# Gating branch of a two-layer RWKV-7 / gMLP step interleaved with the first pair's front, and triangles inverted by blocks of 16 with quadrant matmuls

## The chip, the core and the metric

The kernel runs on one core of one Trainium2 chip. The metric is the time of one execution on the device, in microseconds, as the median of several runs; three runs of the kernel before took 3381.95, 3382.55 and 3396.24 us.

## What is computed

Two layers over 640 tokens (128 of a context, 512 of a latent grid), D_MODEL = 1024, 16 heads of 64. What matters of the reference, per layer (`z = h @ w_in` after a modulated RMSNorm):

```python
def _rwkv_step(S, inp):
    r, w, k, v, neg_kk, b = inp
    sa = jnp.einsum('dbhij,dbhj->dbhi', S, neg_kk)
    S = S * w[..., None, :] + sa[..., :, None] * b[..., None, :] + v[..., :, None] * k[..., None, :]
    return S, jnp.einsum('dbhij,dbhj->dbhi', S, r)
...
    wd = jnp.tanh(wd.reshape(B, T, N_DIR, W_LORA).astype(f32))
    w_logit = p['w0'][l][:, None, None, :] + jnp.einsum('btdr,drc->dbtc', wd, p['w_up'][l])
    decay = jnp.exp(-DECAY_SCALE * jax.nn.sigmoid(w_logit))
...
def chunk_mlp_branch(zu, zv, p, l):
    B, T, _ = zu.shape
    u = jax.nn.gelu(zu)
    v = jax.nn.gelu(zv).astype(jnp.float32)
    mu = jnp.mean(v, axis=-1, keepdims=True)
    var = jnp.mean(jnp.square(v - mu), axis=-1, keepdims=True)
    v = (v - mu) * lax.rsqrt(var + EPS) * p['ln_v_g'][l]
    vc = v.reshape(B, T // CHUNK, CHUNK, H_B, HEAD_B)
    s = jnp.einsum('hpq,bnqhc->bnphc', p['w_s'][l], vc) + jnp.transpose(p['b_s'][l])[:, :, None]
    y = u * s.reshape(B, T, D_B).astype(u.dtype)
    return y @ p['w_branch_b'][l]
...
    mixed = (jax.nn.sigmoid(z_ga) * y_a + jax.nn.sigmoid(z_gb) * y_b) @ p['w_out'][l]
    x = x + g1 * mixed
    h2 = rmsnorm(x, p['norm2_g'][l]) * (1 + sc2) + sh2
    x = x + g2 * (jnp.square(jax.nn.relu(h2 @ p['w1'][l])) @ p['w2'][l])
```

The scan runs forward and backward. The kernel does it by chunks of L = 64 tokens, 10 chunks for each of two directions, for 8 pairs of heads.

## The kernel before

All activations lie as 8 tiles of 128 channels by 640 tokens. A float32 product is done as three passes over operands split in a high and a low part: `load_w` (L97) brings 256 KB of weights through SyncE's queue, ScalarE writes the high part (`hi`, L101), VectorE or GpSimdE the rest (`lo`, L103), and `dense` (L116) runs two `load_w` and 2 x 24 = 48 matmuls of 320 columns (L111, tile `dps`). Such a set of 48 is called a dense block here.

A layer goes through these stages in the program:

- `p1` (L393 to L519): the low-rank inputs (`lah`, `lal`), the gate's v (L491, four quarters of 120 matmuls of 256 columns, evicted with Gelu, tiles `v0` to `v4`), eight dense blocks for u (L504, evicted with Gelu to `uts`), 40 low-rank units in between (`lora_units`, L449: six matmuls, two ScalarE evictions of 320 columns at L468 or L470, one store to `ld`), the normalisation of v, and eight spatial products (`spatial`, L438: five matmuls with `wst`, then VectorE, result to `bd`). In layer 0 it also reduces 32 columns of the modulation (`mod_col`, L162), two reductions of 1024 elements each on VectorE (L168), which the loads of 512 KB feed.
- the front of pair 0, alone: `krv(0, 0, 1, 2)`, `run(0, ...)`, two `gate` blocks.
- the loop over the pairs: `back(i)` (ten recurrence steps, the tiles `pu`), and in between the steps pieces of `front(i + 1)`, dense blocks for k, r, v of the pairs to come (`krv`) and dense blocks of the output gates (`gate`). `SP` (L35) says how many pieces go where: `n` per step, `gn` gate blocks per pair. `mark`, `adv` and `high_priority` give the pieces of a front a higher priority; from that and the program's order the framework orders each engine's queue. Every engine then runs its queue in order.
- `branch_b` (the gate's product with `w_branch_b`), then output projections and the feed-forward part.

`front(i)` (L581) makes, per direction, the decay sums (`cum`, `E`), the operands `LA`, `BK`, then g = BK^T LA per chunk and head (L644, tile `g`), whose masked parts go to `GR`, `LA`, `D` and `TT`. The lower triangles of the 64x64 blocks are inverted: the two 32x32 diagonal blocks of all 20 chunks and both heads at once on VectorE, by substitution over s = 1 to 30 (L673 to L678, tiles `D`, `X`: one multiply and one add each of (31 - s) x s elements), then transposed (`XT`, `XN`, L692 and L694), copied to `TT` (L698), and merged with the off-diagonal block by 2 x 40 small matmuls (tiles `pw`, L705 and L715). `lnexp` (L551) issues Ln and Exp under one table set that is loaded ahead (`pre`).

```python
for s in range(1, 31):
    n = 31 - s
    t3 = tm[:, 0:n * s].rearrange("p (a b) -> p a b", b=s)
    nc.vector.tensor_tensor(t3, AA[:, s + 1:32, s:s + 1].to_broadcast([128, n, s]),
                            X[:, s:s + 1, 0:s].to_broadcast([128, n, s]), ALU.mult)
    nc.vector.tensor_tensor(X[:, s + 1:32, 0:s], X[:, s + 1:32, 0:s], t3, ALU.add)
```

## Time and profile before

| | us |
|---|---|
| median of three runs | 3382.55 |
| the profiled execution | 3388.05 |
| its span, first to last instruction | 3386.3 |
| TensorE busy (matmuls) | 3159.4 |
| VectorE busy | 2145.6 |
| ScalarE busy | 1511.6 |
| GpSimdE busy | 612.4 |
| mean granted TensorE clock, of full | 0.942 |

The profile's page names engines PE (matmuls), PEld (weight loads), DVE (VectorE), ACT (ScalarE), POOL (GpSimdE), SP (SyncE, whose queue issues the loads and stores). L111 is line 111 of the kernel before. The times of matmuls are modelled: they overlap, so a busy share near one is not the engine at its peak; how long a run of matmuls takes is read from the start of the first to the start of what follows. PEclk is the mean granted clock of a stretch; its two levels are 1.2 and 2.4 GHz. The stages of the text are windows in microseconds from the span's start: layer 0's opening 74.6 to 247.4, pair 0's front to 368.0, the loop to its last recurrence matmul at 1074.2; layer 1's 1754.1, 1914.6, 2036.0 and 2743.7.

### The profile page before, as it was taken

The page shows a single profiled execution, that of the slowest core. Times are in us where ns is not written, and L with a number is a line of the kernel's source. Part 1 is how long each engine was busy: PE and PEld are TensorE (multiplying, and loading weights), DVE is VectorE, ACT ScalarE, POOL GpSimd, SP SyncE. Part 2 cuts the span into 40 slices and gives each one's busy share as a digit, 9 for nine tenths or more (in the row PEclk, how much of TensorE's full clock was granted, in tenths as well). Part 3 has the DMA queues.
Part 4 walks back from the last instruction along what each step waited for, and adds up shares of the span by engine and source line. Part 5 has one row for each costly group of instructions (what it writes and reads, how often), then busy time and mean ns, then how long its engine had stood idle before and what let it go on. Part 6 is the DMA issues. An engine that isn't in the chain of part 4 may idle for free.

```text
span 3386.3 us, 66312 instructions
## 1 busy us (share of the span) xinstructions
PE 3159.4 (93%) x26160; PEld 2862.3 (85%) x26160; DVE 2145.6 (63%) x4147; ACT 1511.6 (45%) x3268; POOL 612.4 (18%) x616
## 2 busy tenths in 40 slices
PE   7998899999999999999989979999999999999998
PEld 7897677777778989999989967777777789899998
DVE  7777778887785469933353487788787735532234
ACT  5444445554445354224254434445544543541432
POOL 3004333333231000000000133333323210000000
PEclk8998889998899999999999989899889999999999
DMA  6683112221224536622344522122222245222223
GB/s 210 220 291 102 56 61 72 77 74 61 66 77 138 199 104 205 216 83 75 99 135 139 188 75 66 56 73 77 68 68 72 86 137 184 84 76 75 75 75 106
DMA packets 215671, 372.73 MB, mean 110 GB/s; under 512 B 63680, under 2 KB 72000, under 8 KB 215360
## 3 DMA queue, kind: packets, MB, share of 16 engines
q1 hardware_dynamic: 215360, 368.49, 33.8%
q8 instruction: 206, 3.38, 0.4%
q14 instruction: 105, 0.86, 0.1%
HBM read 288.41 MB, written 63.31 MB: 104 GB/s over the span
## 4 chain that ended last, share of the span: by engine, by line
PE 65%; DVE 18%; DMA 5%; issue 5%; ACT 4%; POOL 3%; SPq 1%; DVEq 0%; ACTq 0%; POOLq 0%
PE dps L111 40%; PE g L644 4%; DMA wada<-in_wada 3%; PE dps L256 3%; PE dps L491 2%; DVE X L678 2%; DVE D L676 2%; PE pu L776 2%; DVE wjunk L168 2%; PE pu L757 2%; PE pu L789 1%; PE pu L795 1%; PE pu L751 1%; DVE lo L103 1%; POOL BK L625 1%
## 5 line engine op out<-in xcount | busy, mean ns | idle before, releaser
L101 ACT ACTIVATE hi<-raw 128x512 fp32r<-128x512 f32 x630 | 397.2, 632 | 1025.6 <-PE dps L111 864.0
L103 DVE TENSOR_TENSOR lo<-raw,hi 128x512 fp32r<-128x512 f32 x550 | 392.1, 714 | 545.9 <-ACT hi L101 526.7
L111 PE MATMUL dps<-ah,hi 128*128 128x320 f32 x2768 | 686.9, 324 | 8.4 <-ACT up L468 5.4
L111 PE MATMUL dps<-ah,lo 128*128 128x320 f32 x2768 | 674.3, 321 | 14.5 <-DVE lo L103 14.5
L111 PE MATMUL dps<-al,hi 128*128 128x320 f32 x2768 | 674.9, 321 | 0.0
L111 PEld LDWEIGHTS dps<-ah,lo 128*128 128x128 f32 x2768 | 474.4, 193 | 29.5 <-DVE lo L103 16.5
L111 PEld LDWEIGHTS dps<-ah,hi 128*128 128x128 f32 x2768 | 474.2, 192 | 28.2 <-ACT up L468 6.0
L111 PEld LDWEIGHTS dps<-al,hi 128*128 128x128 f32 x2768 | 473.9, 192 | 12.7 <-issue 0.8
L168 DVE CUSTOM_DVE_ANT_0 wjunk<-wada,sc 128x1024 f32<-128x1024 f32 x176 | 220.9, 1255 | 33.2 <-DMA wada<-in_wada 30.9
L785 POOL TENSOR_TENSOR sw<-SV,wc 64x128 f32<-64x128 f32 x288 | 150.7, 523 | 439.0 <-DVE SV L803 422.5
L644 PE MATMUL g<-LA,BK 64*128 64x128 f32 x1280 | 193.6, 332 | 32.9 <-DVE LA L656 15.9
L103 POOL TENSOR_TENSOR lo<-raw,hi 128x512 fp32r<-128x512 f32 x80 | 123.2, 1540 | 543.6 <-ACT hi L101 491.8
L644 PEld LDWEIGHTS g<-LA,BK 64*128 64x128 f32 x1280 | 162.0, 226 | 64.6 <-issue 22.2
L111 PE MATMUL dps<-fh,lo 128*128 128x320 f32 x896 | 205.5, 311 | 6.2 <-DVE lo L103 6.0
L111 PE MATMUL dps<-fh,hi 128*128 128x320 f32 x896 | 204.7, 310 | 0.0
L111 PE MATMUL dps<-fl,hi 128*128 128x320 f32 x896 | 204.5, 309 | 0.0
L676 DVE TENSOR_TENSOR D<-AA,X 128x30 f32<-128x30 f32 (+14 forms) x480 | 178.1, 371 | 21.6 <-POOL X L671 11.7
L678 DVE TENSOR_TENSOR X<-X,D 128x30 f32<-128x30 f32 (+14 forms) x480 | 179.9, 375 | 11.3
L249 POOL TENSOR_TENSOR al<-nt,ah 128x320 fp32r<-128x320 f32 x24 | 25.2, 1053 | 728.1 <-ACT ah L248 727.0
L111 PEld LDWEIGHTS dps<-fh,lo 128*128 128x128 f32 x896 | 150.0, 188 | 7.9 <-DVE lo L103 7.8
L625 POOL TENSOR_TENSOR BK<-ta,cum 64x640 f32<-64x640 f32 x64 | 125.8, 1966 | 141.4 <-DVE ta L616 116.3
L111 PEld LDWEIGHTS dps<-fh,hi 128*128 128x128 f32 x896 | 150.3, 188 | 0.0
(293 smaller groups left out, 5798.1 us busy)
## 6 DMA issues: line engine op xcount, KB each, us to landing
raw<-in_w SPq DMA_DIRECT2D x280, 256.0 KB, 2.6
raw<-in_win SPq DMA_DIRECT2D x234, 256.0 KB, 2.7
wada<-in_wada SPq DMA_DIRECT2D x88, 512.0 KB, 4.1
ld<-up SPq DMA_DIRECT2D x80, 320.0 KB, 3.6
th<-ld SPq DMA_DIRECT2D x32, 320.0 KB, 2.9
ta<-ld SPq DMA_DIRECT2D x32, 320.0 KB, 3.0
gd<-spill SPq DMA_DIRECT2D x32, 320.0 KB, 2.3
raw<-in_wo SPq DMA_DIRECT2D x40, 256.0 KB, 2.6
```

Source lines behind the costliest of these rows:

```text
L101: nc.scalar.activation(hi, raw, AF.Copy)
L103: (eng or nc.vector).tensor_tensor(lo, raw, hi.bitcast(F32), ALU.subtract)
L111: nc.tensor.matmul(ps[:, n, 0:HT], w[:, k * 128:(k + 1) * 128], xk[:, n * HT:(n + 1) * HT], start=(first and k == 0 and j == 0), stop=(las ...
L168: nc.vector.tensor_tensor_reduce(junk, wt, sc_cur[0][:, v, :], 1.0, 0.0, ALU.mult, ALU.add, mods[l][:, j, v:v + 1])
L256: nc.tensor.matmul(ps[:, n, 0:HT], w[:, k * 128:(k + 1) * 128], x[:, 4 * kb + k, hs(n)], start=(kb == 0 and k == 0 and j == 0), stop=(kb = ...
L491: nc.tensor.matmul(o, x[:, k, tk * 128:(tk + 1) * 128], w[:, kk * 256:(kk + 1) * 256], start=(k == 0 and j == 0 and tk % 2 == 0), stop=(k ...
L625: nc.gpsimd.tensor_tensor(b[s, c, 1 - h, :], rt[s], e[s], ALU.mult)
L644: nc.tensor.matmul(gs[h][:, c - c0, :], b[s, c, :, :].rearrange("p x t -> p (x t)"), la[s, c, h:h + 2, :].rearrange("p x t -> p (x t)"), s ...
L676: nc.vector.tensor_tensor(t3, AA[:, s + 1:32, s:s + 1].to_broadcast([128, n, s]), X[:, s:s + 1, 0:s].to_broadcast([128, n, s]), ALU.mult)
L678: nc.vector.tensor_tensor(X[:, s + 1:32, 0:s], X[:, s + 1:32, 0:s], t3, ALU.add)
L757: nc.tensor.matmul(pu[s, d, 3, :], SV[:, us[d], h, :], GR[d][:, cs[d], h, :], start=False, stop=True, skip_group_check=True)
L785: nc.gpsimd.tensor_tensor(sw[s], SV[s, both, h, :], wcu[s, both].unsqueeze(2).to_broadcast([64, 2, L]), ALU.mult)
```

## The change

- **The opening.** `p1` moves behind the definitions of front and back. It now computes the low-rank inputs, then k, r, v of pair 0 (`krv(0, 0, 1, 2)`), 20 low-rank units in one piece, the first five pieces of pair 0's front, then the four quarters of v with five low-rank units and three pieces of the front after each; then the normalisation, k and r of pair 1, and the spatial products with two pieces of the front ahead of each. The weights and biases of a spatial product come one head at a time, through one buffer each (`wst`, `bsb`), instead of all heads at once.
- **The eight u blocks** become fillers: they stand first in the list that `gate` takes from, are spilled to `zud` without Gelu, and `gn` now places 24 of them in the loop instead of 16 in front and loop. The Gelu of u, its product with the spatial result and the split for `branch_b` (`branch_b_prep`) stand in the steps of the last pair.
- **Layer 0's late modulation** is done in the loop by halves of 512 elements, one half column a step (`mod_halves`, `mod_some(1)`), 64 loads of 256 KB through one buffer (`wah`).
- **The inversion.** VectorE's substitution runs over the 16x16 diagonal blocks only, s = 1 to 14, two blocks in one instruction of 2 x (15 - s) x s elements. The off-diagonal 16x16 block of each 32x32 block comes from 80 matmuls of 16 columns (`pwa`), a masked add into `wq`, 80 matmuls (`pwt`) and 40 matmuls (`pwn`) of 32 columns, each on one of the four 32x32 quadrants; then the old merge to 64.
- Some tiles of the odd pairs move to a pool that opens after the opening (`rwb`), and the scratch memory for dynamic DMA gets smaller, to make room.

```diff
-SP = {'n': (3, 2, 1, 2, 2, 1, 0, 0, 3, 1), ... 'gn': (2, 2, 2, 1, 2, 2, 2, 1)}
+SP = {'n': (3, 2, 1, 2, 2, 1, 1, 1, 1, 1), ... 'gn': (2, 3, 3, 3, 3, 3, 3, 2)}
...
+        idq = G([128, 32], "idq")
+        for q in range(4):
+            nc.vector.tensor_copy(idq[32 * q:32 * q + 32, :], ident[32 * q:32 * q + 32, 32 * q:32 * q + 32])
+        low16 = G([128, 1], "low16")
+        nc.vector.tensor_reduce(low16, idq[:, 16:32], mybir.AxisListType.X, ALU.add)
...
+                    wq = rw.tile([128, 20, 32], F32, tag="wq", name="wq")
+                    nc.gpsimd.tensor_copy(wq[:, :, 16:32], idq[:, 16:32].unsqueeze(1).to_broadcast([128, 20, 16]))
...
-                        for s in range(1, 31):
...
+                        for s in range(1, 15):
+                            n = 15 - s
+                            t4 = tm[:, 0:2 * n * s].rearrange("p (a t s) -> p a t s", a=2, s=s)
+                            nc.vector.tensor_tensor(t4, xb[:, :, s + 1:16, s:s + 1].to_broadcast([128, 2, n, s]),
+                                                    xb[:, :, s:s + 1, 0:s].to_broadcast([128, 2, n, s]), ALU.mult)
+                            nc.vector.tensor_tensor(xb[:, :, s + 1:16, 0:s], xb[:, :, s + 1:16, 0:s], t4, ALU.add)
...
+                        quads = [slice(32 * q, 32 * q + 32) for q in range(4)]
+                        pw = psr.tile([128, 20, 16], F32, tag="g", name="pwa")
+                        for u in range(20):
+                            for s in quads:
+                                nc.tensor.matmul(pw[s, u, :], D[s, u, :], XN[s, u, 0:16], start=True, stop=True)
+                        nc.vector.scalar_tensor_tensor(wq[:, :, 0:16], pw, low16, idq[:, 0:16].unsqueeze(1).to_broadcast([128, 20, 16]), ALU.mult, ALU.add)
+                        yield "W"
+                        for x in range(2):
+                            us = slice(10 * x, 10 * x + 10)
+                            pt = psr.tile([128, 10, 32], F32, tag="g", name="pwt")
+                            pn = psr.tile([128, 10, 32], F32, tag="g", name="pwn")
+                            for u in range(10 * x, 10 * x + 10):
+                                for s in quads:
+                                    nc.tensor.matmul(pt[s, u - 10 * x, :], wq[s, u, :], XT[s, u, :], start=True, stop=True)
+                            for u in range(10 * x, 10 * x + 10):
+                                for s in quads[0::2]:
+                                    nc.tensor.matmul(pn[s, u - 10 * x, :], XT[s, u, :], wq[s, u, :], start=True, stop=True)
+                            for s in quads[0::2]:
+                                nc.scalar.activation(XN[s, us, :], pn[s], AF.Copy)
+                            for q, s in enumerate(quads):
+                                o = 32 * (q % 2)
+                                nc.scalar.activation(TT[s, us, o:o + 32], pt[s], AF.Copy)
+                        yield "V"
...
+                    fillers = [(27 + m, zud[m]) for m in range(8)] + [(43 + 8 * x + m, gd[x, m]) for x in range(2) for m in range(8)]
...
+                        krv(0, 0, 1, 2)
...
+                        def spatial(h):
+                            ws = p1.tile([128, 128], F32, tag="wst", name="wst")
+                            nc.sync.dma_start(ws, I["wsT"][l, :, h])
+                            bs = p1.tile([128, 128], F32, tag="bsb", name="bsb")
+                            nc.sync.dma_start(bs, I["bs"][l:l + 1, h].to_broadcast([128, 128]))
...
+                        lora(20)
+                        run(0, 5)
+                        for q in range(4):
...
+                            lora(5)
+                            run(0, 3)
...
+                        krv(1, 0, 1)
+                        for h in range(NK):
+                            run(0, 2)
+                            spatial(h)
+                        run(0)
...
+                            nc.scalar.activation(u, u, AF.Gelu_apprx_tanh)
+                            nc.vector.tensor_tensor(t, t, u, ALU.mult)
                             split(bh[m], bl[m], t)
...
+                                for j in range(32):
+                                    wt = rwb.tile([128, 512], F32, tag="wah", name="wah")
+                                    nc.sync.dma_start(wt, I["wada"][0, 16 + j, :, w])
...
+                                mod_some(1)
+                                if i == NPAIR - 1:
+                                    if step == 0:
+                                        branch_b_tiles()
+                                    if step < NK:
+                                        branch_b_prep(step)
```

How the queues read at three places. First TensorE in layer 0, where pair 0's first g matmuls stand (tile `g`; line numbers are those of each kernel). Before:

```order
L111 MATMUL dps<-ah,hi 128x320 x2
L111 MATMUL dps<-al,hi 128x320 x2
L644 MATMUL g<-LA_2793,BK_2794 128x128 x8
L111 MATMUL dps<-ah,lo 128x320 x2
L111 MATMUL dps<-ah,hi 128x320 x2
```

And now:

```order
L862 MATMUL dps<-hi,al 128x256
L862 MATMUL dps<-hi,ah 128x256
L526 MATMUL g<-LA_1157,BK_1158 128x128 x8
L862 MATMUL dps<-hi,ah 128x256
L862 MATMUL dps<-lo,ah 128x256
```

The g matmuls of pair 0 stood among gate blocks (320 columns), after the whole opening; now they stand among the matmuls of the gate's v (256 columns, now L862), inside it.

Second SyncE's queue in layer 0, at the spatial products (`wst` weights, `bsb` biases, `bd<-st` the store of a result). Before, where both were loaded, once:

```order
L303 DMA zs_589<-zraw 32x448
L304 DMA zs_589<-zraw 32x448
L426 DMA bsb<-in_bs 128x1024
L428 DMA wst<-in_wsT 128x1024
L99 DMA raw<-in_win 128x512
```

And now:

```order
L811 DMA bsb<-in_bs 128x128
L809 DMA wst<-in_wsT 128x128
L820 DMA bd<-st 128x640
L811 DMA bsb<-in_bs 128x128
L809 DMA wst<-in_wsT 128x128
L820 DMA bd<-st 128x640
L811 DMA bsb<-in_bs 128x128
L104 DMA raw<-in_win 128x512
```

One load of each for all heads became a load of each per head, between the stores of the heads before. On TensorE the spatial products of six heads stand there one behind the other, with no dense matmul between.

Third ScalarE in the loop, at the normalisation of a pair's result (`YD<-pg` is Ln, `YD<-YD` is Exp). Before:

```order
L718 ACTIVATE TT_3559<-pw_4506 32x10x32 x2
L553 ACTIVATE YD<-pg,c_gn 128x320 x2
L733 ACTIVATE SV<-trv 64x3x64
L553 ACTIVATE YD<-YD 128x640
L735 ACTIVATE SV<-trv 64x4x64
```

And now:

```order
L106 ACTIVATE hi<-raw 128x512
L435 ACT_TABLE_LOAD
L435 ACTIVATE YD<-pg,c_gn 128x320 x2
L435 ACT_TABLE_LOAD
L435 ACTIVATE YD<-YD 128x640
L106 ACTIVATE hi<-raw 128x512
```

Ln and Exp followed each other under one table set; now each has a table load ahead of it, here and at the normalisation of kk in every front. The whole queue holds 29 table loads before and 91 now.

## Rows read from the trace of the kernel before

**Rows 1.** Busy time of each engine by stage, with counts, clock, DMA share, GB/s.

```profile
74.60:247.40 172.80, 162.22 (x1185) 155.72 (x1186) 131.22 (x218) 83.91 (x169) 1.36 (x1) 0.98 0.77 257
247.40:368.00 120.60, 92.67 (x706) 86.12 (x704) 98.00 (x159) 49.40 (x103) 47.40 (x39) 0.85 0.30 94
368.00:1074.20 706.20, 660.51 (x6815) 538.16 (x6817) 538.68 (x1185) 350.34 (x931) 229.25 (x242) 0.92 0.24 76
...
1754.10:1914.60 160.50, 159.46 (x1185) 155.09 (x1186) 51.86 (x83) 77.07 (x157) 1.29 (x1) 0.98 0.47 161
1914.60:2036.00 121.40, 92.68 (x706) 86.00 (x704) 98.03 (x159) 49.38 (x103) 47.85 (x39) 0.84 0.29 93
2036.00:2743.70 707.70, 661.40 (x6815) 538.78 (x6817) 540.12 (x1185) 350.48 (x931) 226.69 (x242) 0.92 0.24 75
```

**Rows 2.** Waits of TensorE, pair 0's front of layer 1: total us, times, longest.

```profile
PE pw L705 <- DVE XN L694: 16.5, 1, 16.5
```

**Rows 3.** Waits of TensorE, loop of layer 1.

```profile
PE pw L705 <- DVE XN L694: 11.1, 7, 3.4
```

**Rows 4.** The page's costliest groups: the substitution; busy us, mean ns, idle before.

```profile
L676 DVE TENSOR_TENSOR D<-AA,X 128x30 f32<-128x30 f32 (+14 forms) x480 | 178.1, 371 | 21.6 <-POOL X L671 11.7
L678 DVE TENSOR_TENSOR X<-X,D 128x30 f32<-128x30 f32 (+14 forms) x480 | 179.9, 375 | 11.3
```

**Rows 5.** The chain that ended last, whole span: start us, us, engine, tile, line.

```profile
363.08 2.37 PE pw L705 x80
...
1772.78 14.58 PE dps L491 x120
...
1889.05 7.04 PE dps L111 x48
```

**Rows 6.** The same chain, 1875 to 1912 us (opening of layer 1).

```profile
1896.09 0.89 PE dps L463 x6
...
1899.61 1.11 PE dps L443 x10
```

**Rows 7.** The same chain, 2300 to 2400 us (loop of layer 1).

```profile
2306.69 0.55 PE pg L578 x2
...
2345.53 1.79 PE g L644 x15
...
2356.32 0.38 PE pu L757 x8
...
2394.24 1.45 PE pw L705 x80
```

**Rows 8.** TensorE in order of time, 2313 to 2326 us: start, us, instruction.

```profile
2315.75 1.04 PE L730 MATMUL trv<-ident,vp 128*128 128x128 f32 x8
```

**Rows 9.** TensorE in order of time, 2368 to 2382 us.

```profile
2373.82 0.41 PE L111 MATMUL dps<-al,hi 128*128 128x320 f32 x1
2374.16 0.45 PE L789 MATMUL pu<-psb,TT 64*64 64x64 f32 x8
```

**Rows 10.** Costliest groups of ScalarE, whole span: the low-rank evictions.

```profile
L468 ACT ACTIVATE up<-hps,dpar 128x320 f32<-128x320 f32 x64 | 30.7, 543 | 0.2
```

**Rows 11.** DMA issues, whole span: count, KB each, median us to landing.

```profile
SV<-in_st SPq DMA_DIRECT2D x64, 16.0 KB, 2.1
...
wst<-in_wsT SPq DMA_DIRECT2D x2, 512.0 KB, 4.7
```

**Rows 12.** VectorE's substitution by shape, loop of layer 1.

```profile
L678 DVE TENSOR_TENSOR X<-X,D 128x108 f32<-128x108 f32 x14 | 4.1, 293 | 0.4
...
L676 DVE TENSOR_TENSOR D<-AA,X 128x30 f32<-128x30 f32 x14 | 2.9, 205 | 4.9 <-POOL X L671 4.7
```

**Rows 13.** ScalarE in order of time, 1078.5 to 1085 us.

```profile
1080.24 1.28 ACT L553 ACT_TABLE_LOAD   x1
1081.54 0.95 ACT L553 ACTIVATE YD<-pg,c_gn 128x320 f32<-128x320 f32 x2
```

**Rows 14.** The page's costliest groups: the reductions of the modulation.

```profile
L168 DVE CUSTOM_DVE_ANT_0 wjunk<-wada,sc 128x1024 f32<-128x1024 f32 x176 | 220.9, 1255 | 33.2 <-DMA wada<-in_wada 30.9
```

More of the change, by code (lines that the diff above doesn't have):

```diff
@@ L699, in front @@
-                        yield "mrg"
+                        nc.vector.transpose(XN.rearrange("p u j -> p j u"), xa.rearrange("p t j -> p j t"))
+                        nc.scalar.activation(vp[1][:, 64:64 + T], v[:, ::-1], AF.Copy)
+                        bon = kd[0]
+                        nc.vector.tensor_tensor(bon, kd[0], kd[1], ALU.add)
+                        nc.vector.scalar_tensor_tensor(bon, bon, P[:, RKC + i:RKC + i + 1], r, ALU.mult, ALU.mult)
+                        ps = dense_ps()
@@ new lines, in front @@
+                        f32mm(ps, ones_b, bon)
+                        nc.vector.tensor_tensor(pv(bon), ps[:, :, 0:HT], pv(v), ALU.mult)
+                        nc.sync.dma_start(bvd[i], bon)
+                        yield "bon"
+                        quads = [slice(32 * q, 32 * q + 32) for q in range(4)]
[3 more added lines that the diff above has]
+                                nc.tensor.matmul(pw[s, u, :], D[s, u, :], XN[s, u, 0:16], start=True, stop=True)
@@ L714, in front @@
                                     s = slice(64 * h + 32, 64 * h + 64)
-                                    nc.tensor.matmul(pw[x][64 * h:64 * h + 32, u - 10 * x, :], wsb[s, u * 32:(u + 1) * 32], XT[s, u, :], start=True, stop=True)
+                                    nc.tensor.matmul(pw[x][64 * h:64 * h + 32, u - 10 * x, :], wsb[s, u * 32:(u + 1) * 32], TT[s, u, 32:64], start=True, stop=True)
                             for h in range(2):
@@ L843, in drain @@
                             pass
-                    gates = [(x, m) for x in range(2) for m in range(8)]
+                    fillers = [(27 + m, zud[m]) for m in range(8)] + [(43 + 8 * x + m, gd[x, m]) for x in range(2) for m in range(8)]
                     gi = 0
@@ L854, in gate @@
                         nonlocal gi
-                        for _ in range(min(n, len(gates) - gi)):
+                        for _ in range(min(n, len(fillers) - gi)):
                             mark("gate")
-                            gate_block(*gates[gi])
+                            spill_block(*fillers[gi])
                             gi += 1
```

380 lines of the change are left out of this document (182 added, 198 removed).

## The prediction, made blind

> **What bounds the kernel now.** I first cut the span into stages by when each stage's own matmuls run, and asked for the busy time of every engine in each [rows 1]. A layer has an opening (gating and low-rank work), a front of pair 0 that nothing accompanies, a loop over the pairs up to the last recurrence matmul, and a rest that the change hardly touches. The reader is to see three regimes. In the opening of layer 1 TensorE is busy 159.46 of 160.50 us at a clock of 0.98. In pair 0's front it is busy 92.68 of 121.40 at 0.84. In the loop it is busy 661.40 of 707.70 at 0.92, while VectorE has 540.12. So the loop looks TensorE-bound, but a busy matmul there is not one at its peak.
>
> The waits say who holds TensorE. In the front one wait of 16.5 us stands out: the merge waits for the transposes behind the 30-step substitution on VectorE [rows 2]. In the loop the same wait comes 7 times but costs 11.1 us in all [rows 3], of the 46 us that TensorE idles. The substitution is 480 multiplies and 480 adds, 178.1 + 179.9 us over 16 pairs, 22.4 us a pair [rows 4].
>
> Then unit prices, at the upper of the two clock levels. A dense block is 48 matmuls in 7.04 us, 0.147 each, and a quarter of the gate's v 14.58 [rows 5]; a low-rank unit 0.89, a spatial product 1.11 [rows 6]. In the loop a recurrence group of 8 takes 0.38, 15 g matmuls 1.79, two ones_b products 0.55, 80 merge matmuls 1.45 [rows 7]; 8 transposes 1.04 [rows 8]. One dense matmul between two recurrence groups takes 0.34 from its start to the next start [rows 9], so an insertion costs some 0.19 beyond the matmul, about 0.1 of it already inside the 0.38.
>
> With the counts of the program's order, the loop of a layer (first trv to last pu) needs: 1603 dense x 0.147 = 235; 392 recurrence groups x 0.38 = 149; 560 g instructions x 0.119 = 67; 316 transposes x 0.13 = 41; 108 ones_b instructions x 0.275 = 30; 14 merges x 1.45 = 20; some 300 insertions x 0.1 = 30. That is **572 us, against 706.20 and 707.70 measured: 134 us of slack**. It holds the 46 us of idle time, the lower clock, and gaps too short to be listed.
>
> **Part by part, per layer.**
> *Opening and pair 0's front.* Now 172.80 + 120.60 = 293.4 us in layer 0 and 160.50 + 121.40 = 281.9 in layer 1. The eight u blocks and two gate blocks leave (10 x 7.04 = 70 us of TensorE). What stays, run as one stretch: five k, r, v blocks 35; 40 low-rank units 36; the gate's v 58; 8 spatial products 9; pair 0's g 10, transposes 3, ones_b products 2, merges 3, new quadrant matmuls 4 (below); 90 shape changes 9. Sum 169. To it I add stalls. (a) The first 20 low-rank units now stand in one piece: ScalarE needs two evictions of 0.543 each [rows 10], 1.09 a unit against TensorE's 0.89, and has weight splits and pair 0's exponentials in the same queue: 12 us. (b) The spatial weights come through one buffer, so every product waits for a load issued after the product before it. The nearest rows are loads of 16 KB, 2.1 us, and the old one of 512 KB, 4.7 [rows 11]; 64 KB is nearer the first, so I take 2.4 with the issue, and six of eight products stand without dense work between: 14 us (bounds 12 and 28). (c) Of the front's other idle time, 28.7 - 16.5 = 12 us [rows 1, 2], half: 6. Together **201 us**, a gain of 92 and 81. The 16.5 us wait goes because the low-rank and v matmuls lie over the front; if that cover fell short, the shorter substitution still takes some 15 off it.
>
> *The inversion.* VectorE loses 22.4 us a pair and gains 28 instructions of 28 to 112 elements at 0.205 (128x30) to 0.293 (128x108) [rows 12], 7.3 us, and one masked add, 0.4: 14.7 us less a pair. In the loop this lies beside TensorE, and I count only what follows from it (the slack). TensorE gains 80 matmuls of 16 columns and 120 of 32, two instructions each: 400. The merge has two row groups at work and takes 1.45 us for 80 instructions [rows 7], 18 ns each; 320 of the new ones have four quadrants, so I take half, 9 ns: 2.9 + 1.4 = **4.3 us a pair**. Bounds: 3, and at the lower clock 2.37 us for 80 [rows 5], 11.9.
>
> The merge's rows show two row groups sharing one PSUM bank without taking turns. The Trainium skill (TensorEngine Tiling (Array Packing), Gotcha 1: PSUM Pressure) says that different row tiles cannot access the same PSUM bank simultaneously, and here all four write one bank. By it the new matmuls would take turns, and the sum would be that of the fourth rival; the merge's rate speaks against it.
>
> *The loop.* It takes on 454 more dense matmuls (by the order, 2057 against 1603), 67 us, and 7 x 4.3 = 30 of quadrants; shape changes stay. TensorE's own need goes from 572 to **669**. The slack I take at 70 instead of 134: VectorE, busy 538.68 of 706.20, loses some 85, so masks and weight splits come sooner, and nearly every pair has 288 dense matmuls to lay over waits instead of 182 to 240. In the opening of layer 1, where dense work is plentiful, 1 us is idle [rows 1]; the bounds are 15 and 134. Loop: 739, **33 us more** than now.
>
> *ScalarE.* The order holds 91 table loads instead of 29: Ln and Exp, which shared one set, now load one each, four loads a pair. A load takes 1.28 us, and the next instruction starts 0.02 after it [rows 13]: 5.1 us a pair in a loop where ScalarE is busy 350 of 706. I cost it at nothing beyond the slack, because dense matmuls stand behind nearly every recurrence step; uncovered, it is the third rival. The Trainium skill (ScalarE: Activation LUTs, What ACT_TABLE_LOAD costs) puts a drain of about 1.38 us on top of each load, by which the third rival would end at 3476, slower; the trace has no room for such a drain.
>
> *Rest.* 74 dense matmuls pass from before to after the last recurrence: 11 us. Layer 0's late modulation moves into the loop, 64 halves with two reductions of half of 1.255 [rows 14], 80 us of VectorE that lay under the opening's matmuls and takes back most of what the substitution freed there: 8 us (0 to 25; its loads, through one buffer, stand in SP's queue ahead of weight loads, which is in the 25).
>
> **Sum.** Layer 0: -92 + 33 + 11 + 8 = -40. Layer 1: -81 + 33 + 11 = -37. The profiled execution took 3388.05 us, 5.5 above the median of 3382.55; less 77 it is 3311, and the median **3306 us**. With the slack between 45 and 100 and the opening 10 either way, the forecast's own range is 3236 to 3386.
>
> **The rivals.**
> 1. *The loop swallows the moved blocks.* If VectorE is what keeps TensorE waiting there, the slack falls to about 20: 2 x 50 less, **3206 us**. For it: VectorE's 76% in the loop. Against: short waits on recurrence and evictions stay. Chance 0.20.
> 2. *The loop's slack stays.* It is TensorE's in-order queue waiting for the recurrence and for g's evictions, which a dense block placed elsewhere in the order does not cover; then everything moved in is paid in full: 2 x 64 more, **3434 us**, slower. It decides from a slack of 108 a layer. For it: only 11 of the 46 us belong to the substitution [rows 3]. Chance 0.10.
> 3. *Table loads on the chain.* All 64 in the pairs delay the recurrence or its normalisation: 64 x 1.28 = 82 us more, **3388 us**, no change. Against: ScalarE is half idle. Chance 0.10.
> 4. *The quadrants take turns.* Two row groups together reach 18 ns, so one at a time takes 36: 400 x 36 ns = 14.5 us a pair instead of 4.3, on the bound engine, 163 more: **3469 us**. Chance 0.04.
>
> **How the numbers follow.** The forecast has the remaining 0.56. A measurement of this kernel tells about 0.5%, 17 us, from no change: 3366 and 3400 are the borders. Faster: nine tenths of 0.56, the first rival and a little of the third, 0.72. Same: the rest of the forecast and most of the third, 0.14. Slower: the second and the fourth, 0.14. The range 3215 to 3395 leaves out the two slow rivals and a third of the first, 0.2.
>
> **What would show it.** Opening and front together near 201 us, with gaps of 2 to 3 us ahead of the spatial products; no long wait ahead of the quadrant matmuls, and 80 of them in well under 1.45 us; 28 substitution instructions of 0.2 to 0.3; a loop of 730 to 750 us with a granted clock above 0.92. A loop over 780, or quadrant bursts of 3 us, would make the prediction wrong on one side, a loop of 700 on the other.

## The result, and the profile after

The changed kernel takes 3837.76 us (median of four runs, 3830.84 to 3881.17) where the kernel before takes 3382.25: a ratio of 1.136, 95% interval 1.127 to 1.145. It is 455 us slower; the forecast was 77 us faster, and the range ended at 3395. The profiled execution took 3881.17 us, the longest of the four, so its trace is 493 us longer than the one of before: 471 in the stages below, 22 in the rest.

The page of the changed kernel: span; busy time, share and instructions of TensorE and VectorE; the granted clock in 40 slices.

```profile
span 3879.5 us, 79239 instructions
PE 3537.9 (91%) x32560; PEld 3162.2 (82%) x32560; DVE 1986.0 (51%) x3773; ACT 1635.2 (42%) x3476; POOL 609.7 (16%) x650
PEclk8787868787777999999997878788889889999999
```

VectorE has lost work, as the change meant it to (1986 us busy against 2145.6). TensorE's clock is low in both openings and loops (the first 13 slices, and slices 22 to 34). The stages, cut as in [rows 1], but with opening and front as one window, since the change interleaves them:

```profile
74.60:355.90 281.30, 230.16 (x1761) 201.24 (x1761) 98.41 (x162) 118.26 (x250) 29.91 (x30) 0.76 0.32 108
355.90:1337.00 981.10, 892.75 (x10069) 741.59 (x10069) 592.66 (x1268) 422.32 (x1050) 251.17 (x266) 0.79 0.26 83
2025.00:2302.50 277.50, 224.40 (x1761) 195.90 (x1760) 99.00 (x162) 115.50 (x242) 30.31 (x24) 0.78 0.33 110
2302.50:3222.70 920.20, 837.28 (x10069) 700.16 (x10070) 498.04 (x1000) 419.63 (x1046) 234.82 (x265) 0.86 0.22 69
```

From such a row three parts can be worked out: idle time (length less PE busy), what the low clock cost (length x (1 - PEclk), since the lower level is half speed), and the rest, TensorE's work at full clock. The page gives the clock to two places, so the last two are good to some 5 us in a loop.

| stage | | length | idle | clock | rest |
|---|---|---|---|---|---|
| opening and front, layer 0 | before | 293.4 | 38.5 | 21.5 | 233 |
| | after | 281.3 | 51.1 | 67.5 | 163 |
| opening and front, layer 1 | before | 281.9 | 29.8 | 22.6 | 230 |
| | after | 277.5 | 53.1 | 61.1 | 163 |
| loop, layer 0 | before | 706.2 | 45.7 | 56.5 | 604 |
| | after | 981.1 | 88.4 | 206.0 | 687 |
| loop, layer 1 | before | 707.7 | 46.3 | 56.6 | 605 |
| | after | 920.2 | 82.9 | 128.8 | 709 |

The rest moved as forecast: 66 to 71 us left each opening, 83 to 104 came into each loop. What was not forecast is the idle time and, more than that, the clock: 0.79 and 0.86 in the loops where the prediction wanted above 0.92. The loop's slack did not fall from 134 to 70 us a layer; idle time and clock alone went from 103 to 212 in layer 1 and to 294 in layer 0.

Where the clock is low, one pattern stands out. TensorE in order of time, changed kernel, layer 1's opening (start, us, instruction, count):

```profile
2221.39 0.31 PE L592 MATMUL pwt<-XT,wq 32*32 32x32 f32 x2
2221.63 0.64 PE L116 MATMUL dps<-al,hi 128*128 128x320 f32 x1
2222.20 0.31 PE L592 MATMUL pwt<-XT,wq 32*32 32x32 f32 x2
2222.44 0.64 PE L116 MATMUL dps<-al,hi 128*128 128x320 f32 x1
```

and three windows there: the low-rank units in one piece, pair 0's quadrants and merge, the spatial products.

```profile
2056.20:2076.70 20.50, 13.95 (x60) 12.55 (x60) 5.25 (x6) 11.30 (x24) 0.88 (x1) 0.50 0.77 267
...
2208.30:2247.40 39.10, 37.65 (x506) 25.79 (x508) 4.95 (x7) 12.02 (x23) 1.69 (x2) 0.52 0.14 44
2255.60:2295.30 39.70, 21.23 (x101) 18.90 (x100) 9.88 (x16) 8.51 (x11) 1.52 (x2) 0.61 0.28 86
```

One dense matmul and two quadrant instructions take 0.81 us from one start to the next; in a block a dense matmul takes 0.147 at the upper clock [rows 5] and 0.27 at the lower (2683.99 to 2686.65 us of this trace). One pair's quadrants and the first third of its merge, priced at 4.3 and 1 us, take 39 here together with some 50 dense matmuls, at a clock of 0.52 and with TensorE "busy" nearly throughout.

### The profile page after: what moved, and what is told of

Same layout as the page of the kernel before. It is cut to its first block, busy times and chain, and to the rows that moved or that the text cites. A ratio compares the mean times of both kernels' runs of the same rounds, so it can differ in the third digit from the quotient of the medians.

```text
span 3879.5 us, 79239 instructions
## 1 busy us (share of the span) xinstructions
PE 3537.9 (91%) x32560; PEld 3162.2 (82%) x32560; DVE 1986.0 (51%) x3773; ACT 1635.2 (42%) x3476; POOL 609.7 (16%) x650
## 5 line engine op out<-in xcount | busy, mean ns | idle before, releaser
L116 PE MATMUL dps<-ah,lo 128*128 128x320 f32 x2768 | 717.7, 337 | 61.2 <-DVE lo L108 59.6
L116 PE MATMUL dps<-ah,hi 128*128 128x320 f32 x2768 | 727.7, 340 | 4.7 <-ACT hi L106 1.8
L116 PE MATMUL dps<-al,hi 128*128 128x320 f32 x2768 | 726.2, 339 | 0.0
L116 PEld LDWEIGHTS dps<-ah,lo 128*128 128x128 f32 x2768 | 501.8, 203 | 81.5 <-DVE lo L108 63.6
L116 PEld LDWEIGHTS dps<-ah,hi 128*128 128x128 f32 x2768 | 501.1, 203 | 27.5 <-ACT hi L106 3.3
L116 PEld LDWEIGHTS dps<-al,hi 128*128 128x128 f32 x2768 | 500.9, 202 | 20.9 <-issue 2.9
L694 DVE COPY SV<-pu 64x128 f32<-64x128 f32 x160 | 46.8, 294 | 249.7 <-ACT SV L693 223.8
L116 PEld LDWEIGHTS dps<-fl,hi 128*128 128x128 f32 x896 | 150.3, 188 | 0.0
L173 DVE CUSTOM_DVE_ANT_0 wjunk<-wada,sc 128x1024 f32<-128x1024 f32 x112 | 142.7, 1274 | 14.2 <-DMA wada<-in_wada 13.0
L706 DVE TENSOR_TENSOR SV<-pu,sw 64x128 f32<-64x128 f32 x256 | 73.6, 288 | 136.3 <-PE pu L698 130.3
```

What stands on the lines that cost most here:

```text
L116: nc.tensor.matmul(ps[:, n, 0:HT], w[:, k * 128:(k + 1) * 128], xk[:, n * HT:(n + 1) * HT], start=(first and k == 0 and j == 0), stop=(las ...
L173: nc.vector.tensor_tensor_reduce(junk, wt, sc_cur[0][:, v, :], 1.0, 0.0, ALU.mult, ALU.add, mods[l][:, j, v:v + 1])
L694: nc.vector.tensor_copy(SV[64:128, both, 1, :], pu[64:128, :, 1, :])
L706: nc.vector.tensor_tensor(dst, pu[s, :, 2, :], sw[s], ALU.add)
```

## The experiments

"Half-clock time" in the expectations is the time at the lower of the clock's two levels, twice the clock column above. "Pieces" are stretches of merge and quadrant matmuls in TensorE's program order with no other matmul between. All ratios are to the kernel before, run on the same chip.

| run | median us | ratio, 95% interval | pieces |
|---|---|---|---|
| before | 3382 to 3389 | 1 | 32 |
| the change | 3837.76 | 1.136 (1.127 to 1.145) | 276 |
| change, old inversion | 3575.73 | 1.056 (1.054 to 1.059) | 32 |
| before, quadrants | 3851.00 | 1.138 (1.134 to 1.141) | 596 |
| before, quadrants in fixed bursts | 3699.02 | 1.093 (1.090 to 1.095) | 112 |
| before, quadrants in priority bursts | 3512.05 | 1.038 (1.034 to 1.041) | 80 |
| change, priority bursts | 3745.36 | 1.108 (1.104 to 1.112) | 81 |
| change, short substitution only | 3643.61 | 1.077 (1.074 to 1.081) | 220 |
| before, short substitution only | 3494.51 | 1.032 (1.030 to 1.034) | 248 |
| the same, merge in bursts | 3374.94 | 0.995 (0.992 to 0.997) | 32 |
| before, merge in bursts | 3368.49 | 0.994 (0.992 to 0.996) | 30 |

### Is it the inversion or the schedule?

The changed kernel with the 30-step substitution back (the lines of the kernel before, same pieces of a front, no quadrants):

```diff
-                        for s in range(1, 15):
...
+                        for s in range(1, 31):
...
-                        pw = psr.tile([128, 20, 16], F32, tag="g", name="pwa")
...
```

> The changed kernel with the old inversion: VectorE's 30-step substitution and no quadrant matmuls; the schedule, the pieces of a front and everything else stay as in the change. Theory A (the quadrant matmuls and the merge are a stretch of small matmuls in which the granted clock falls to its lower level, about 25 to 35 us in each pair of the changed kernel's loop): without the 400 small matmuls the half-clock time of a layer's loop falls from 266 us (layer 1) towards the 115 of before, and the kernel gains about 7 us of quadrants and 8 of clock a pair, some 240 us: about 3600. Theory B (where the dense blocks stand in the order makes the loop long; what inverts the triangles matters little): only the quadrants' own 7 us a pair go, less what VectorE's 15 us a pair give back: 3740 to 3840, and the half-clock time of the loop stays above 220 us.

and the kernel before with the new inversion alone (and the smaller scratch memory, for room):

```diff
-                            if s % 5 == 0:
+                            if s % 4 == 0 or s == 14:
                                 yield "sub"
...
+                        pw = psr.tile([128, 20, 16], F32, tag="g", name="pwa")
...
-    nc = _bacc.Bacc("TRN2", target_bir_lowering=False, num_devices=1)
+    nc = _bacc.Bacc("TRN2", target_bir_lowering=False, num_devices=1, dynamic_dma_scratch_size=2048)
```

> The kernel before with the new inversion alone (blocks of 16 and quadrant matmuls, as many pieces of a front as before); opening, gating and fillers stay as before. Theory A: every pair gets the stretch of small matmuls with little dense work beside it; 16 times about 7 us of quadrants and 5 to 8 of clock, less the 22 us of waits ahead of the merge in the two loops and 30 in the two fronts alone: 3500 to 3570, half-clock time of the loop above 180 us. Theory B: 16 x 4.3 = 69 us of quadrants, less up to 52 of waits: 3380 to 3410, half-clock time of the loop near 115.

Layer 1's loop, first the change with the old inversion, then the kernel before with the quadrants:

```profile
2104.50:2927.10 822.60, 742.54 (x7308) 616.86 (x7308) 598.28 (x1221) 406.95 (x994) 244.76 (x259) 0.91 0.25 77
```

```profile
2251.70:3211.80 960.10, 910.57 (x9706) 719.32 (x9705) 469.87 (x995) 372.72 (x998) 229.31 (x254) 0.75 0.18 57
...
2564.10:2639.20 75.10, 75.10 (x794) 54.05 (x783) 8.36 (x25) 17.15 (x40) 6.19 (x12) 0.50 0.08 24
```

Theory A has both signs, but only the first size: 3576 without the quadrants (it had about 3600), 3851 with nothing but them, where it had 3500 to 3570. In the second run one pair's quadrants and merge, with the matmuls that stand between them, fill 75.1 us at half clock. The loop's rest is 670, 65 more than before: 9 us for 61 more dense matmuls that stand in it now, and 8 us a pair. The clock costs 240. The new schedule without quadrants still loses 190 us; its loop's rest, 669, is 64 above before's 605, which is the moved blocks' price (67).

### Are they slow as such, or by where they stand?

In program order one or two quadrants stood between single dense matmuls and recurrence groups. First, all bursts of the run with the quadrants made whole as fixed pieces:

```diff
+                        with tc.tile_critical():
                             for u in range(20):
                                 for s in quads:
...
```

> The kernel before with the new inversion (as in the run with the quadrants only), but every burst of quadrant matmuls (80; 40 and 20, twice) and of the merge (4 x 40) stands as one piece in TensorE's order, where dense matmuls and recurrence groups stood between single quadrants. Theory A1 (small matmuls alone bring the clock down, however they stand): half-clock time of a loop stays above 300 us, and the time above 3650. Theory A2 (it is the order: one dense matmul between two quadrants stretches the low-activity stretch to 58 to 75 us and pays a switch each time): a pair pays the bursts' 6 to 10 us and little more; half-clock time of a loop under 220 us, 3450 to 3550.

3699: the half-clock time of layer 1's loop falls from 480 to 279 us, between the theories; the time itself is on A1's side. But each fixed piece brought a branch and its own waits, and idle time rose from 50 to 101 us. So the same by priority:

```diff
-                        with tc.tile_critical():
+                        with tc.high_priority(offset=3000):
                             for u in range(20):
...
```

> The kernel before with the new inversion, and a priority offset of 3000 instead of 200 around the bursts of quadrant and merge matmuls, so that in TensorE's order each burst stands as one piece (144 pieces in the program, as 16 pairs need, where the run with the quadrants only has 548), without the edges of its own that the run with fixed pieces had. Theory A2 (dense matmuls and recurrence groups between single quadrants are the price): 16 x 4.3 to 6.5 us of bursts less the 52 us of waits ahead of the merge, 3400 to 3450, half-clock time of a loop under 200 us. Theory A1 (small matmuls bring the clock down however they stand): above 3550, half-clock time of a loop above 270 us.

(Counted as in the table, the pieces are 80 against 596.)

Layer 1's loop, and TensorE in order of time at one pair's first burst:

```profile
2096.00:2868.50 772.50, 718.67 (x9677) 594.93 (x9675) 465.97 (x990) 367.29 (x993) 231.28 (x254) 0.89 0.23 70
```

```profile
2580.16 1.53 PE L710 MATMUL pwa<-XN,D 32*32 32x16 f32 x160 [1.24 <-DVE XN L695]
2581.62 0.45 PE L809 MATMUL pu<-SV,LA 128*64 128x64 f32 x8
```

3512, between the two forecasts: the order of the same instructions is worth 339 us, three quarters of the loss. The half-clock time is under A2's 200 us in layer 1 (170) and over it in layer 0 (221). Whole, 160 instructions take 1.46 us to the next start, 9 ns each, and the loop's rest is 634, 29 more than before: 5 us for 32 more dense matmuls, and 3.5 us for each of seven pairs (2.3 in layer 0), where 4.3 were forecast. Some 126 us stay, much of it clock (0.89 and 0.86 in the loops), so A2 has the larger part and A1 a share. In the changed kernel the same edit does less:

> The changed kernel with the same priority offset around its quadrant and merge bursts, nothing else. Theory A2: the quadrants cost 4.3 to 7 us a pair over the run with the old inversion (3576), and VectorE's relief gives some of it back: 3580 to 3680. Theory A1: 3750 or more.

3745, 92 us less, and at A1's bound: with the new schedule the quadrants cost 170 us over the old inversion even in whole bursts. Summed over the four stages, some 70 of it is TensorE's own work (16 x 4.3 = 69 were forecast), 60 the clock and 20 idle time.

### Less work, and slower

The quadrants taken out, with the short substitution kept, so that the off-diagonal 16x16 blocks are left out of the inverse; first in the changed kernel, then in the kernel before:

```diff
-                        quads = [slice(32 * q, 32 * q + 32) for q in range(4)]
...
+                        for q in range(4):
+                            s = slice(32 * q, 32 * q + 32)
+                            o = 32 * (q % 2)
+                            nc.scalar.activation(TT[s, :, o:o + 32], XT[s, 0:20, :], AF.Copy)
                         yield "W"
```

> The changed kernel without its quadrant matmuls: VectorE's short substitution stays, the off-diagonal 16x16 blocks are left out of the inverse. It is the new schedule with VectorE relieved, and differs from the run with the old inversion only by VectorE's 15 us a pair. If VectorE is what makes the loop's waits (first rival of the prediction): 100 us under that run, below 3480, with under 50 us of TensorE idle in a loop. If it is TensorE's in-order queue (second rival): 3540 to 3580, with 65 us or more idle in a loop.

> The kernel before with the short substitution and without quadrant matmuls (the same part of the inverse left out): old schedule, VectorE relieved. The waits ahead of the merge go, 11 us a loop and 16 a front: 3330 if nothing takes their place; 3290 or less if VectorE held up more than the merge; 3370 to 3390 if another wait takes over.

Both came out where no theory had put them: 3644, 68 above the run with the full substitution, and 3495, 110 above the kernel before, with less for VectorE to do and no more for TensorE. The second one's layer 1 loop:

```profile
2066.50:2857.80 791.30, 744.95 (x6917) 598.24 (x6917) 469.72 (x988) 360.80 (x948) 230.71 (x256) 0.85 0.23 69
```

VectorE has 70 us less to do than in [rows 1], TensorE idles 46 as before, and the clock is 0.85 instead of 0.92. The order shows a difference: the merge stands in 248 pieces instead of 32. A reading of it, not tested by itself, is that the framework places the merge as soon as its inputs are ready, and without the long substitution ahead that is while dense matmuls and recurrence groups are ready as well. This edit also moves the marks between the pieces of a front; in the changed kernel they stay where the run with the old inversion has them, and the merge breaks up there too, into 220 pieces against 32. To test whether the pieces are the price, the merge alone put into whole bursts:

```diff
+                            with tc.high_priority(offset=3000):
                                 for u in range(10 * x, 10 * x + 10):
                                     for h in range(2):
...
```

> The kernel before with the short substitution and without quadrant matmuls (the off-diagonal 16x16 blocks left out, as in the run without the bursts, 3494), and the merge in whole bursts by the priority offset. Theory A2: without dense matmuls between single merge matmuls the loops' half-clock time falls from 230 to 130 us or less, the loops from 791 to 720 to 740: 3365 to 3410. If the loss has another cause (VectorE's or GpSimdE's new instructions): 3450 or more.

```profile
1998.90:2722.10 723.20, 676.00 (x6893) 552.68 (x6892) 471.58 (x988) 356.12 (x946) 236.46 (x256) 0.91 0.25 75
```

3375, 120 us less for the same instructions, and without one quadrant matmul in the kernel. The last run below has the same bursts and the long substitution, 3368. The priority by itself is worth 20 us there, where the pieces hardly change, so some 100 of the 120 are the pieces; and VectorE's relief brings nothing in this schedule.

### The smaller parts

The table set of Ln and Exp loaded again behind the opening and each SiLU (41 loads in the order instead of 91):

```diff
                         odd[0] = rwb
+                        preload()
...
+                                preload()
                                 for j in range(32):
```

> The changed kernel with the shared table set of Ln and Exp loaded again behind the opening and behind each SiLU of the late modulation, so that Ln and Exp of the pairs share one set again: 41 table loads in the order instead of 91. If table loads on the recurrence's chain were the loss (theory C): 50 x 1.28 = 64 us faster or more, about 3770. Theories A and B: within 20 us of the changed kernel, 3815 to 3845.

3804.96 (1.126, 1.119 to 1.133): 33 us, half of what theory C asks and 10 below the range of A and B. The runs of the two kernels overlap at the edge; in the profiles 56 us off layer 0's loop and 22 off layer 1's.

The spatial weights whole:

```diff
-                            ws = p1.tile([128, 128], F32, tag="wst", name="wst")
-                            nc.sync.dma_start(ws, I["wsT"][l, :, h])
...
+                        ws = p1.tile([128, NK, 128], F32, tag="lah", name="wst")
+                        nc.sync.dma_start(ws, I["wsT"][l])
```

> The changed kernel with the spatial weights and biases of all heads loaded at once, into the low-rank inputs' dead buffers, so that no spatial product waits for a load behind the product before it. All theories: the 33 us that seven products take in the opening of layer 1 shrink to under 12, in both layers: 40 to 60 us faster, 3780 to 3800, and the loops do not change by more than 10 us.

3829.21 (1.130, 1.125 to 1.136), 9 us where 40 to 60 were expected. What it aimed at was there: in the changed kernel the line of these products waited

```profile
its engine sat idle before it (us, times) until:
  DMA wst<-in_wsT: 28.9, 8
```

(the 28.9 adds up the waits of weight loads and of matmuls; TensorE itself sat idle 18.5 of the 39.7 us above), and the 80 instructions, 40 us before, take 13.8. But the median moved less than the stall: the gain is 43 us between the two profiled executions and 9 between the medians, and no run here tells which of them it is.

The u blocks back in the opening (also after each quarter of v), 16 fillers left in the loop, with the old inversion and the two edits above; then with the merge's priority as well:

```diff
-                        lora(20)
+                        for _ in range(4):
+                            lora(5)
+                            gate(1)
                         run(0, 5)
...
```

> The changed schedule's opening with the eight u blocks back in it, as dense cover: after each five of the first 20 low-rank units and after each quarter of v; gate blocks in the loop as before (16), old inversion, shared table set and whole spatial weights as in the two runs before. Opening and front of a layer together need 169 - 4 + 56 = 221 us of TensorE and I expect 235 to 255 where the kernel before takes 282 to 293; the loops as before (707), layer 0's with some 25 us for the late modulation: 3385 - 40 - 45 + 30 = 3330 (3300 to 3390), faster than both kernels. If the loop's loss in the run with the old inversion does not come from the moved blocks, the loops stay above 780 and the time above 3420.

> The run with the u blocks back in the opening, with the priority offset around the merge bursts. There the merge of pair 0 alternated with single dense matmuls for 36 us at the lower clock in each layer's opening. Theory A2: that stretch shrinks to 10, some 25 us less a layer, and the loops hardly change: 3440 to 3470. Theory A1: within 15 us of 3510.

3510.10 (1.037, 1.035 to 1.039) and, with the merge in bursts, 3484.44 (1.030, 1.026 to 1.033). The first missed its forecast by 180 us; the second fell by 26 us, half of what A2 had for two layers, and met neither theory. Opening and front of layer 0 take 273.6 us at a clock of 0.95 in the second, where 235 to 255 were expected. Layer 1's loop is within 33 us of before's, layer 0's is not (second run):

```profile
348.20:1163.50 815.30, 734.62 (x6985) 604.17 (x6985) 661.70 (x1488) 376.15 (x961) 250.40 (x251) 0.85 0.30 94
...
2107.70:2848.20 740.50, 681.44 (x7004) 556.30 (x7003) 577.68 (x1222) 367.84 (x955) 235.86 (x251) 0.93 0.26 80
```

So the same without the late modulation, whose 32 columns are left at zero:

```diff
+                            if not l:
+                                nc.vector.memset(mods[0][:, 16:48], 0.0)
+                            return
```

> The run with u in the opening and the merge in bursts, without layer 0's late modulation (64 loads of 256 KB, 128 half reductions; the 32 columns are left at zero). There layer 0's loop took 815 us against 740 in layer 1. Theory (b): layer 0's loop falls to 735 to 750, the kernel to 3400 to 3430. If it is the order of the two layers that differs by chance: layer 0's loop stays above 780, 3450 or more.

```profile
352.00:1097.50 745.50, 689.99 (x7004) 563.56 (x7003) 575.47 (x1222) 367.61 (x955) 236.54 (x251) 0.92 0.26 80
```

3416.11 (1.008, 1.005 to 1.011): the late modulation costs 70 us in that loop, 25 of idle time and 63 of clock, less 18 of rest. Which part of it does so is not shown, since the run takes out VectorE's reductions (661.70 us busy to 575.47) and the loads together. TensorE's longest wait there, the merge for VectorE, halved (with and without the modulation; us in total, times, longest):

```profile
PE pw L585 <- DVE XN L563: 16.6, 7, 10.1
...
PE pw L585 <- DVE XN L563: 7.5, 7, 1.3
```

SyncE's queue is held up as well, as the changed kernel's loop of layer 0 shows (same columns):

```profile
SPq L929 <- DVE mod L933: 92.1, 16, 16.5
SPq L929 <- DVE macc L933: 69.1, 20, 14.4
```

In 36 cases one of its 64 loads waits at the head of the queue until VectorE has reduced the one before it; weight loads stand behind.

The gate blocks away from the pair's end, in the run with the old inversion:

```diff
+                                if step in (5, 8) and ng > 1:
+                                    gate(1)
+                                    ng -= 1
```

> The changed schedule with the old inversion, and two of a pair's three gate blocks moved from the pair's end to its sixth and ninth recurrence steps. Theory (a): TensorE's waits for low parts of weights (30 us in layer 1's loop) fall under 12, idle time of a loop from 80 to under 60, the half-clock time with it: loops 25 to 45 us shorter each, 3490 to 3525. If the moved blocks cost their full price wherever they stand: 3560 to 3590.

How such a wait comes about is seen in the changed kernel, where TensorE waits 5.2 us for a low part at a pair's end. VectorE there (start, us, instruction):

```profile
2675.72 1.84 DVE L486 TENSOR_SCALAR th<-th 128x640 f32<-128x640 f32 x1
2677.48 2.17 DVE L730 SCALAR_TENSOR_TENSOR yc<-yc,par,gs 128x640 f32<-128x640 f32 x1
2679.57 2.55 DVE L488 TENSOR_TENSOR_SCAN cum<-scanm,th 128x640 f32<-128x640 f32 x1
2682.04 0.66 DVE L108 TENSOR_TENSOR lo<-raw,hi 128x512 fp32r<-128x512 f32 x1
```

The run went the other way, 3626.84 (1.070), 51 us slower. The waits for low parts did go (30.2 us in layer 1's loop of the run it is built on, 0.0 now), but others took their place, so that the idle time stayed (80.1 us, then 78.4), and the clock fell from 0.91 to 0.87:

```profile
L518 PE MATMUL g<-LA,BK 64*128 64x128 f32 x560 | 104.2, 380 | 21.7 <-DVE LA L530 19.4 <-issue 2.4
L579 PE MATMUL pw<-XN,TT 32*32 32x32 f32 x560 | 11.3, 199 | 12.2 <-DVE XN L558 12.2
```

Theory (a) falls.

### Versions

All the repairs on the change at once:

> The change with all that the runs found mended: bursts by priority, the shared table set, whole spatial weights, two gate blocks of a pair at its sixth and ninth steps. From the run with the bursts (3745): less 33 for the tables, 10 to 40 for the spatial products, 50 to 90 for the gates if theory (a) holds: 3590 to 3650. If (a) falls: 3670 to 3710. Under 3385, as forecast for the change, only if the parts hinder one another in ways that no run has shown.

3637.26 (1.073, 1.070 to 1.077): 200 us of the 455 come back. It lies in the range that was given for the case that theory (a) holds, which it did not, so that match is luck. The change does not win with any set of repairs tried. The one part that gained was pair 0's front, so the new inversion for pair 0 only:

```diff
+                        if i == 0:
...
+                        else:
```

> The kernel before, with the new inversion in bursts for pair 0 of each layer alone (its front has no cover for the wait of 16.5 us behind the long substitution), the old one for the other seven pairs, and the priority offset around all bursts. If theory A2 holds, the fronts give 16.5 + 16.5 back less 2 x 5 of bursts, and the loops stay at 706 to 708: 3350 to 3370, faster than the kernel before. Theory A1: the front's quadrants give it all back, 3375 to 3400.

> The run with the new inversion for pair 0 alone, with one of a pair's two gate blocks moved from the pair's end to its sixth recurrence step. That run gained 16 and 22 us ahead of the loops and lost 26 and 17 in them. If dense work clumped at the pair's end is what its loops lost, they fall by 10 each: 3360 to 3375, faster than the kernel before. If not: 3380 to 3400.

3391.13 (1.002, 1.001 to 1.004) and 3417.77 (1.009, 1.006 to 1.012). The first gave 16 and 22 us ahead of the loops, as A2 had it, and lost 26 and 17 in them, where 74 more dense matmuls now stand (11 us) at a clock of 0.90 and 0.91; so its time is in A1's range, for another reason than A1's. One gate block moved (`if step == 5 and ng > 1: gate(1)`) made that worse. Last, the priority around the merge alone, in the kernel before, the edit of two lines shown above:

> The kernel before with the priority offset around the merge bursts alone. There the merge already stood nearly whole (32 pieces in the order, 30 now), so by theory A2 nothing changes but the order around: 3375 to 3395. If the priority itself is what the loops of the pair-0 run lost: 3410 to 3430, loops of 725 to 735.

```profile
378.60:1084.60 706.00, 666.03 (x6841) 539.73 (x6839) 545.40 (x1188) 350.17 (x931) 219.64 (x240) 0.91 0.24 74
...
2046.30:2740.30 694.00, 650.01 (x6841) 526.40 (x6839) 545.45 (x1188) 350.39 (x931) 220.43 (x240) 0.94 0.25 76
```

3368.49, a ratio of 0.994 (0.992 to 0.996), below the 3375 to 3395 expected: the only version here with the whole computation that is faster than both kernels, by 0.6%. Its openings are slower than before's and its loops faster; with 30 pieces against 32, the cause is open.

## Why the prediction was wrong

**The work was summed rightly.** Opening and front: 169 us of TensorE's work forecast, 163 measured. The loop: 97 more forecast, 83 and 104 measured. Quadrants in a burst: 9 ns each forecast, 9 measured; so the fourth rival (they take turns) is out. The Trainium skill (TensorEngine Tiling (Array Packing), Gotcha 1: PSUM Pressure) says that row tiles cannot use one PSUM bank at the same time. The 1.46 us for 160 instructions into one bank show no such turns at the fourth rival's price (36 ns each).

**The step that failed is the slack**: "The slack I take at 70 instead of 134". By the prediction's own sum of 669 us a loop it came out at 312 us in layer 0 and 251 in layer 1. The openings failed by the same fault, with 281 and 278 us against 201. The forecast had three faults.

1. It counted waits and took the clock for a part of them that dense work removes. [rows 1] showed 0.98 in the dense opening and 0.84 in the front alone; the prediction then moved the opening's dense blocks away from 20 low-rank units and eight spatial products without pricing the clock there. It cost 67.5 and 61.1 us where 21.5 and 22.6 stood, and idle time was 51 and 53 where 32 were forecast. That ate the 92 and 81 us of gain and left 12 and 4. In these traces the clock is low where few dense matmuls stand, 0.50 at the low-rank units and 0.61 at the spatial products. Idle time stands there too, and no run parts the two; but the 75.1 us at 0.50 show that it stays low without any.
2. It priced a quadrant by the merge's bursts [rows 7] and took for granted that the quadrants would stand in bursts too. The program order, which can be read without a run, had the changed merge and quadrants in 276 pieces and the old merge in 32, and [rows 9] had the price of an insertion. This is the larger fault: in the changed kernel the new inversion costs 262 us over the old one (3838 against 3576), where 69 were forecast for its quadrants. Whole bursts gave 92 back there; in the kernel before, order alone was worth 339.
3. "VectorE, busy 538.68 of 706.20, loses some 85" in a loop: it lost 42 in layer 1 (540.12 to 498.04), and in layer 0 it gained 54, with the late modulation. The substitution itself gave 101 in layer 1; weight splits (8), the products with u (7) and the masked add (4) took some back, and the rest is spread over operations of the fronts. In the kernel before, with the merge in whole bursts, the short substitution is no faster than the long one (3375, 3368), so the first rival (VectorE keeps TensorE waiting) had nothing to give there. The second rival, that the slack stays, was nearer, but the slack grew, mostly by the clock, and the time went well past its 3434.

**Smaller terms.** The late modulation was put at 8 us, 0 to 25 at most; it costs 70 in the run where it was taken out. The prediction had named both VectorE's load and the loads' place in SyncE's queue, and priced them too low. Table loads were put at nothing: 33 us came back. Spatial products, 9 us and 14 of stalls (bounds 12 and 28): the stage took 39.7, of which 18.5 were idle, within the bounds, and 15 the clock at 0.61, which had no price. The long wait ahead of the merge did go, as forecast: the pair-0 run has 3.6 us of it left in layer 1's front, and gains 16 and 22 us ahead of the loops.

## What to carry to other kernels

Before pricing small matmuls by a row where they stand in a burst, read from the program order whether they will: here a round of one dense matmul and two 32x32 instructions took 0.81 us, where the same in blocks of their own take about 0.3. A step that is made faster on another engine can change the order on the critical one; here a shorter substitution on VectorE broke up the merge on TensorE and cost 110 us until a priority put it together. And a dense block taken out of a stretch gives back less than its price if what is left is poor in dense work: 71 and 66 us of TensorE's work left the openings here, and they became 12 and 4 us shorter.

## What the runs showed of the hardware

- A dense matmul of 320 columns between two pairs of 32x32 instructions: 0.81 us a round at the lower clock level, though two such instructions in a burst take 0.02 (upper level) and the dense one 0.27 (lower level). The Trainium skill (TensorEngine Tiling (Array Packing), Key Properties) says that a change of tiling mode drains TensorE. The trace agrees in so far as a round costs some 0.5 us more than its parts; a drain as such is not seen in it. This was the rule to weigh against the change.
- TensorE can be "busy" for 75.1 of 75.1 us at half clock. Busy time tells nothing of it, the granted clock does. Ahead of that stretch (the kernel before with the quadrants) stood dense blocks and recurrence groups at the upper level, then a wait of 2.05 us for VectorE and the first quadrants:

```profile
2550.00:2564.10 14.10, 12.05 (x143) 10.04 (x142) 12.56 (x33) 4.11 (x10) 2.11 (x3) 1.00 0.18 52
```

- Removing the waits for the low parts of the weights (30.2 us in layer 1's loop) made a kernel 51 us slower: other waits took their place, and the clock cost some 36 us more in that loop.
